# Stick-breaking block of a decoder trunk: prompt heads in two lanes with their own temporaries, transposes laid later behind their scores, 12 page places for 14, columns spread over more steps

## The chip, the cores and the metric

The kernel runs on one core of a Trainium2 chip. The metric is device time in microseconds (us); three unprofiled runs before the change gave 1417.66 us (median), 1416.6 and 1419.02. One more execution was profiled: it took 1419.73 us, and its recorded span, on which every row below is dated, is 1418.0 us.

## The reference, cut to what matters

Two layers run for a prompt group (256 tokens) and a sample group (8 sequences of 8 new tokens). Layer 1 is stick-breaking attention with 16 heads of 64. The samples also attend to a paged cache: 8 pages of 128 past keys each, for each of the 8 sequences.

```python
def sb_block(qb, k, v, q_pos, bias):
    k_pos = jnp.arange(k.shape[1])
    z = jnp.einsum('bqhd,bkhd->bhqk', qb, k).astype(jnp.float32) * (SB_HEAD_DIM ** -0.5)
    z = z + bias.astype(jnp.float32)[None, :, None, None]
    mask = k_pos[None, :] < q_pos[:, None]
    log_rem = jnp.where(mask, jax.nn.log_sigmoid(-z), 0.0)
    rev = lax.cumsum(log_rem, axis=3, reverse=True)
    suffix = jnp.concatenate([rev[..., 1:], jnp.zeros_like(rev[..., :1])], axis=-1)
    att = jnp.where(mask, jnp.exp(jax.nn.log_sigmoid(z) + suffix), 0.0)
    return jnp.einsum('bhqk,bkhd->bqhd', att.astype(v.dtype), v)
...
def odd_mixer(h, w_in, w_out, bias, k_past, v_past):
    b, t, _ = h.shape
    qkv = (h @ w_in).reshape(b, t, 3, SB_HEADS, SB_HEAD_DIM)
...
    return y.reshape(b, t, MIX_WIDTH) @ w_out, k, v
```

## The kernel before, in words

Prompt and sample tokens lie side by side as 320 columns of features. A **column** is one block of 128 output features of a projection: its 512 KB of weights (`raw`) come by one DMA, ScalarE copies them to a rounded high part (`whi`), VectorE forms the low part (`wlo`), and TensorE runs 24 matmuls (8 blocks of features, three products each). `convert_ahead` converts one column ahead of the one that is multiplied and lets `raw` be fetched up to three columns ahead.

`odd_in` first projects the 8 columns of q. Then it walks 18 **steps** `i`. Step `i` does `score` of half sequence `i` (4 key pages, 32 small matmuls into bank `ps`, which the profile shows as two passes each, x64), whose stick-breaking weights (`stick`, a chain over ScalarE and VectorE that ends in an exponential) end up in `s_z`; `value` of half `i-2` (4 value pages, 16 matmuls or x32 in the profile, into `po`); then some of the 16 remaining columns of k and v (`column`; those of v are transposed afterwards by three transposes of `s_vT`); `turn`, which transposes `s_z` of half `i-1` and copies it to `s_at`; and pieces of the prompt's own attention.

How many columns step `i` does is set by `int(COLS * (i + 1))`. The prompt's attention comes in pieces made by `prompt(qb, t0)` and one `new_keys` (the samples' own new keys). A prompt piece does its scores on TensorE (bank `pp`), leaves a chain of some two dozen instructions to ScalarE and VectorE for its two halves in the scratch tile `room`, and yields `LP`, an amount of planned TensorE time after which `steps()` takes the lane up again: four transposes of each half, and 16 value matmuls. `steps()` compares with `pe[0]`, the planner's sum of TensorE time, so `LP` sets the place in TensorE's order, not a time on the chip. In the kernel before there is one lane: a piece begins when the one ahead of it has ended.

The order on TensorE and on SP (the queue that issues the DMAs) is that of the code; on VectorE, ScalarE and GpSimd a scheduler lays it at build time. Each engine works through its own list in order.

The cache comes as 128 **pages** of 512 KB (64 of keys, 64 of values), in the order in which the steps take them. The `PGS` places `pg` are used again and again; nine pages more are put once into tiles that are idle until then (`lend`: `sb_v` 3, `sb_k` 2, `ahi` and `alo` 2 each). Up to `PGS` + 9 pages are fetched before the block starts. From then on `refill` issues the next page in the list right after the matmuls that read a place, and SP waits there for these matmuls. A `raw` is issued from the same queue, behind the pages of its step.

After step 17 the output projection `out_proj` starts (8 columns, `pd`).

Of the kernel before, what the change touches and what calls it, by code (L numbers as in the profile page):

```python
# [10 lines left out]
F32 = mybir.dt.float32  # L11
# [187 lines left out]
def trunk(ctx: ExitStack, tc: tile.TileContext, A, O, phases=None):  # L199
# [26 lines left out]
    def bank(tag="pb", n=None):  # L226
        return own[0].tile([128, 512], F32, tag=tag, name=tag, bufs=n or 5 - own[1])
# [15 lines left out]
    def cc(name):  # L243
        if name in coff:
            at, n = coff[name]
            return cst[:, at:at + n]
        for off, t in (eoff, cste), (soff, csto):
            if name in off:
                at, n = off[name]
                return t[0][:, at:at + n]  # L250
# [3 lines left out]
    def vv(name, i=0, n=1):  # L254
        at, _ = voff[name]
        return vec[:, at + i:at + i + n]
# [12 lines left out]
    def spend(k, m, n, passes):  # L269


        now = (32 if k <= 32 else 64 if k <= 64 else 128, 32 if m <= 32 else 64 if m <= 64 else 128)
        if passes == 0:
            pe[0] += n / 2400 + 0.014
        else:
            pe[0] += passes * max(now[1] / 1200 + 0.004, n / 1200) / (2 if now[1] == 64 else 1)
        if now != shape[0]:
            pe[0] += 0.09
        shape[0] = now

    def mm(out, lhsT, rhs, start=True, stop=True):
        n, m = math.prod(rhs.shape[1:]), math.prod(lhsT.shape[1:])
        spend(lhsT.shape[0], m, n, 0 if lhsT.dtype == F32R else 2)
        nc.tensor.matmul(out, lhsT=lhsT, rhs=rhs, start=start, stop=stop, skip_group_check=True)  # L284

    def tr(out, in_, base=0):
        n = in_.shape[0]
        spend(n, math.prod(in_.shape[1:]), n, 1)
        nc.tensor.transpose(out, in_, ident[base:base + n, base:base + n])
# [3 lines left out]
    def act(out, in_, f=AF.Copy, **kw):  # L293
        if load[0] is not None and f in (AF.Ln, AF.Exp):
            with tc.issue_after(load[0].ins):
                S.activation(out, in_, f, **kw)  # L296
        else:
            S.activation(out, in_, f, **kw)  # L298
# [15 lines left out]
    def stt(out, in0, scalar, in1, op0, op1, eng=None):  # L314
        (eng or V).scalar_tensor_tensor(out, in0=in0, scalar=scalar, in1=in1, op0=op0, op1=op1)  # L315
# [91 lines left out]
    def split(dst, src, scale=1.0):  # L407

        hi, lo = dst
        act(hi, src, scale=scale)  # L410
        stt(lo, src, scale, hi, ALU.mult, ALU.subtract)

    def part(a, *ix):
        return a[0][ix], a[1][ix]
# [1249 lines left out]
    def odd_plan():  # L1664
        return [(A["w_sb"][c], KT) for c in list(range(8)) + [8 * j + t for t in range(8) for j in (1, 2)]] + [(A["w_so"][c], KT) for c in range(KT)]

    PGS = 14
    COLS = 1.8
    GATE = 3
    LP = 9.0  # L1670
    HPO = 300

    class Odd:
# [3 lines left out]
        def __init__(self):  # L1677
            self.made, self.tiles = 0, {}
            self.turn, self.more, self.limit = 0, [], PGS
            self.pool = tc.tile_pool(name="kvr", bufs=1, reuse_waits="tile")  # L1680
# [29 lines left out]
        def fetch(self):  # L1710
# [5 lines left out]
            if lent:  # L1716
                t = self.once.pop(0)
            elif len(self.more) and self.turn >= PGS:
                t = self.more[self.turn - PGS]
            else:  # L1720
                t = self.kvr.tile([128, 1024], F32, tag="pg", name="pg", bufs=PGS)
            if not lent:
                self.turn = (self.turn + 1) % (PGS + len(self.more))
            reg = nc.sync.value_load(pages[0:1, 8 * b + j:8 * b + j + 1], min_val=0, max_val=A["kv"].shape[0] - 1)
# [19 lines left out]
    def odd_in(od, prep, op, ctx):  # L1744
        halves = od.halves
        a = prep.a
        kT, vt = od.kT, od.vt
        qT = op.tile([128, KT, NT], F32, name="sb_q")

        room = op.tile([128, 4, 1024], F32, name="sb_room")  # L1750
        acc = op.tile([128, 8, 64], F32, name="sb_acc")
        new = op.tile([128, KT, 64], F32, name="sb_new")
        ec = op.tile([128, KT, 64], F32, name="sb_ec")
# [6 lines left out]
        st = {}  # L1760
# [5 lines left out]
        def softplus(z, e, l):  # L1766

            act(e, z, AF.Abs)
            act(e, e, AF.Exp, scale=-1.0)
            act(l, e, AF.Ln, bias=1.0)  # L1770
            stt(e, z, 0.0, l, ALU.max, ALU.add)

        def weigh(z, T):
            V.tensor_sub(z, z, T)
            act(z, z, AF.Exp)

        def stick(z, e, l, n, initial=0.0):


            softplus(z, e, l)  # L1780
            one = bc(ones[:, 0:1], [128, n])
            for s in range(0, 512, n):
                V.tensor_tensor_scan(l[:, s:s + n][:, ::-1], data0=one, data1=e[:, s:s + n][:, ::-1],
                                     initial=initial, op0=ALU.mult, op1=ALU.add)
            weigh(z, l)
# [66 lines left out]
            split(part(o, ALL, ALL, slice(NP + 8 * b, NP + 8 * b + 16)), w)  # L1852


        def two(i, p):
            return room[:, i, 512 * p:512 * p + 512]

        def keys(t):
            V.tensor_mul(kT[:, t], dense(a), prep.norm.r)
# [8 lines left out]
                tr(pt[:, tb], vT[:, 128 * tb:128 * tb + 128])  # L1868
            act(vt[:, :, 128 * t:128 * t + 128], pt)

        def prompt(qb, t0):

            n = 128 * (qb + 1)
            H = 512 // n
            qs = slice(128 * qb, 128 * qb + 128)
            rows = [slice(64 * p, 64 * p + 64) for p in range(2)]
            ps = [bank("pp", 2).rearrange("p (h n) -> p h n", h=H) for p in range(2)]
            for j in range(H):
                for p in range(2):
                    mm(ps[p][:, j], qT[rows[p], t0 + j, qs], kT[rows[p], t0 + j, :n])  # L1880
            for p in range(2):
                z = two(0, p).rearrange("p (h n) -> p h n", h=H)
                for j in range(H):
                    b = vv("sb_bias", 2 * (t0 + j) + p)
                    if qb:
                        act(z[:, j, :128], ps[p][:, j, :128], AF.Identity, bias=b)
                    stt(z[:, j, n - 128:], ps[p][:, j, n - 128:], b, cc("causal"), ALU.add, ALU.add)
                stick(two(0, p), two(1, p), two(2, p), n)
            yield LP
            for p in range(2):  # L1890
                pt = bank("pp", 2)
                for j in range(4):
                    s = slice(128 * j, 128 * j + 128)
                    tr(pt[:, s], two(0, p)[:, s])
                act(two(3, p), pt)
                yield 1.0 + p
            py = bank("pp", 2)[:, :128 * H].rearrange("p (t n) -> p t n", n=128)
            for j in range(H):
                for kb in range(qb + 1):
                    for p in range(2):  # L1900
                        h, s = 2 * (t0 + j) + p, n * j + 128 * kb
                        mm(py[rows[p], j], vt[:, kb, 64 * h:64 * h + 64], two(3, p)[:, s:s + 128],
                           start=kb == 0, stop=kb == qb)
            split(part(o, ALL, slice(t0, t0 + H), qs), py)

        def new_keys():

            ps = bank("pp", 2).rearrange("p (t q) -> p t q", t=KT)
            rows = [slice(64 * p, 64 * p + 64) for p in range(2)]
            for t in range(KT):  # L1910
                for p in range(2):
                    mm(ps[rows[p], t], kT[rows[p], t, NP:], qT[rows[p], t, NP:])
            z, e, l = (two(i, 0) for i in range(3))
            for t in range(KT):
                stt(z[:, 64 * t:64 * t + 64], ps[:, t], vv("sb_two", t), cc("win"), ALU.add, ALU.add)
            softplus(z, e, l)
            yield 6.0
            T, all_ = bank("pp", 2), bank("pp", 2)
            mm(T, cc("sufx"), e)
            mm(all_, cc("two64"), e)  # L1920
            weigh(z, T)
            act(ec.rearrange("p t q -> p (t q)"), all_, AF.Exp, scale=-1.0)
            yield 2.0
            pn = bank("pp", 2).rearrange("p (t q) -> p t q", t=KT)
            for t in range(KT):
                for p in range(2):
                    h = 2 * t + p
                    mm(pn[rows[p], t], vt[rows[p], 2, 64 * h:64 * h + 64], z[rows[p], 64 * t:64 * t + 64])
            act(new, pn)
            st["new"] = True  # L1930

        def small():

            for at, g in ((4, prompt(1, 0)), (8, prompt(1, 2)), (8, prompt(0, 0)), (12, prompt(1, 4)),
                          (16, new_keys()), (16, prompt(1, 6)), (16, prompt(0, 4))):
                while st["cols"] < at or st["step"] < GATE:
                    yield None
                yield from g

        lanes = [[small(), 0.0]]  # L1940

        def steps():

# [33 lines left out]
        for i in range(len(halves) + 2):  # L1977
# [7 lines left out]
            if "new" in st:  # L1985
                while ends:
                    finish(ends.pop(0))
            n = max(0, min(16, int(COLS * (i + 1))) - st["cols"])
            steps()
# [77 lines left out]
```

## Time and profile before

| what | value |
|---|---|
| median of 3 runs | 1417.66 us |
| profiled execution, its own time | 1419.73 us |
| span of the profile | 1418.0 us |
| TensorE busy | 1313.9 us (93%) |
| VectorE busy | 901.8 us (64%) |
| ScalarE busy | 661.8 us (47%) |
| DMA | 268.11 MB, mean 189 GB/s |
| scores of step 0 begin | 834.14 us |
| output projection begins | 1046.02 us |

The busy shares are averages over the span. The block that is changed lies between 834 and 1046 us, and what holds it up is read from that stretch alone: which engine waits, for whom, and how busy the DMA engines are. An idle TensorE also shows a lower granted clock afterwards (1.00 in the rows is 2.4 GHz, and a stretch that mixes 2.4 and 1.2 GHz shows a mean between).

### The profile page before, as it was taken

How to read it: one execution, taken by the hardware profiler on the slowest of the kernel's cores; microseconds unless marked ns; L12 is line 12 of the kernel's file. 1: busy time of each engine (PE TensorE's matmuls, PEld its weight loads, DVE VectorE, ACT ScalarE, POOL GpSimd, SP SyncE). 2: the span in 40 equal slices, each digit the busy share in tenths (PEclk: the TensorE clock that was granted, in tenths of full speed). 3: DMA queues.
4: the chain of work that ended last, by engine and by line, in shares of the span. 5: the costliest groups of instructions: out<-in, count | busy, mean ns of one | idle time of the engine just before them, and what ended most of it. 6: DMA issues, size and time to landing. Idle time of an engine off the chain costs nothing.

```text
span 1418.0 us, 28483 instructions
## 1 busy us (share of the span) xinstructions
PE 1313.9 (93%) x10883; PEld 1199.4 (85%) x10883; DVE 901.8 (64%) x1830; ACT 661.8 (47%) x1450; POOL 281.0 (20%) x558
## 2 busy tenths in 40 slices
PE   7799898999999999999999998788689999999997
PEld 6688687887889968999999997676478689999997
DVE  6877787778756545666565656666655455665654
ACT  6645355455436424544344535556444245443443
POOL 6524535435121101111010110000010011110001
PEclk9899998999999999999999999899899999999999
DMA  5333232224437883444757748797997834444443
GB/s 207 119 104 99 89 94 81 87 82 141 145 123 275 309 307 98 152 149 149 249 167 251 269 152 314 253 321 281 408 384 303 299 110 150 149 149 149 149 141 104
DMA packets 81691, 268.11 MB, mean 189 GB/s; under 512 B 9426, under 2 KB 22226, under 8 KB 77074
## 3 DMA queue, kind: packets, MB, share of 16 engines
q1 hardware_dynamic: 64594, 247.30, 50.9%
q10 hardware_dynamic: 16960, 18.98, 4.1%
q8 instruction: 86, 1.41, 0.4%
q14 instruction: 51, 0.42, 0.1%
HBM read 254.35 MB, written 11.90 MB: 188 GB/s over the span
## 4 chain that ended last, share of the span: by engine, by line
PE 60%; DMA 6%; DVE 4%; ACT 3%; issue 1%; SPq 1%; POOL 0%; ACTq 0%; DVEq 0%; POOLq 0%
PE pd L284 33%; PE pe L284 18%; PE pb L284 3%; PE ps L284 2%; DMA mkv<-in_mkv 2%; DMA pg<-in_kv 2%; DMA raw<-in_w_sb 1%; DMA out_memv<-kvt 1%; DVE wlo L358 1%; PE pG L284 1%; PE pR L284 1%; ACT sb_room L296 1%; DVE sb_room L315 1%; PE pp L284 1%; ACT whi L298 1%
## 5 line engine op out<-in xcount | busy, mean ns | idle before, releaser
L298 ACT ACTIVATE whi<-raw 128x512 fp32r<-128x512 f32 (+1 forms) x541 | 308.1, 617 | 381.9 <-PE pd L284 158.9
L358 DVE TENSOR_TENSOR wlo<-raw,whi 128x512 fp32r<-128x512 f32 (+1 forms) x541 | 383.8, 747 | 83.5 <-ACT whi L298 82.1
L284 PE MATMUL pd<-ahi,whi 128*128 128x320 f32 (+2 forms) x1336 | 431.2, 324 | 4.0 <-DVE r_e L1372 1.8
L284 PE MATMUL pd<-ahi,wlo 128*128 128x320 f32 (+1 forms) x1328 | 411.1, 310 | 3.1 <-DVE wlo L358 3.0
L284 PE MATMUL pd<-alo,whi 128*128 128x320 f32 (+2 forms) x1336 | 410.3, 309 | 0.0
L284 PEld LDWEIGHTS pd<-ahi,whi 128*128 128x128 f32 (+1 forms) x1336 | 257.7, 193 | 14.3 <-ACT R L296 2.3
L284 PEld LDWEIGHTS pd<-ahi,wlo 128*128 128x128 f32 x1328 | 257.0, 194 | 5.8 <-DVE wlo L358 4.3
L284 PEld LDWEIGHTS pd<-alo,whi 128*128 128x128 f32 (+1 forms) x1336 | 256.8, 192 | 0.4
L284 PE MATMUL pe<-alo,whi 128*128 128x320 f32 x416 | 129.7, 312 | 0.0
L284 PE MATMUL pe<-ahi,wlo 128*128 128x320 f32 x416 | 129.1, 310 | 0.5 <-DVE wlo L358 0.5
L284 PE MATMUL pe<-ahi,whi 128*128 128x320 f32 x416 | 128.7, 310 | 0.0
L533 POOL TENSOR_TENSOR fw<-fw 128x320 f32<-128x320 f32 x44 | 39.1, 888 | 332.8 <-DVE fw L532 303.5
L434 POOL TENSOR_TENSOR acc<-acc,w 128x320 f32<-128x320 f32 (+1 forms) x48 | 47.7, 994 | 248.2 <-ACT w L298 245.8
L284 PEld LDWEIGHTS pe<-ahi,wlo 128*128 128x128 f32 x416 | 78.1, 188 | 1.5 <-DVE wlo L358 1.4
L284 PEld LDWEIGHTS pe<-alo,whi 128*128 128x128 f32 x416 | 78.1, 188 | 0.5
L284 PEld LDWEIGHTS pe<-ahi,whi 128*128 128x128 f32 x416 | 78.0, 188 | 0.3
L284 PE MATMUL pd<-flo,whi 128*128 128x320 f32 x176 | 54.3, 309 | 0.0
L284 PE MATMUL pe<-fhi,wlo 128*128 128x320 f32 x176 | 54.3, 309 | 0.0
L284 PE MATMUL pd<-fhi,whi 128*128 128x320 f32 x176 | 54.3, 309 | 0.0
L284 PE MATMUL pd<-fhi,wlo 128*128 128x320 f32 x176 | 54.3, 309 | 0.0
L284 PE MATMUL pe<-fhi,whi 128*128 128x320 f32 x176 | 54.3, 309 | 0.0
L284 PE MATMUL pe<-flo,whi 128*128 128x320 f32 x176 | 54.3, 309 | 0.0
(463 smaller groups left out, 2114.0 us busy)
## 6 DMA issues: line engine op xcount, KB each, us to landing
pg<-in_kv SPq DMA_DIRECT2D x119, 512.0 KB, 7.6
raw<-in_w_fi SPq DMA_DIRECT2D x88, 512.0 KB, 3.5
mkv<-in_mkv SPq DMA_DIRECT2D x32, 1024.0 KB, 9.9
raw<-in_w_fo SPq DMA_DIRECT2D x32, 512.0 KB, 3.6
raw<-in_w_sb SPq DMA_DIRECT2D x24, 512.0 KB, 6.8
raw<-in_w_gp SPq DMA_DIRECT2D x16, 512.0 KB, 3.5
raw<-in_w_mk SPq DMA_DIRECT2D x16, 512.0 KB, 3.8
raw<-in_w_mv SPq DMA_DIRECT2D x16, 512.0 KB, 3.6
```

The source lines that it names most:

```text
L284: nc.tensor.matmul(out, lhsT=lhsT, rhs=rhs, start=start, stop=stop, skip_group_check=True)
L296: S.activation(out, in_, f, **kw)
L298: S.activation(out, in_, f, **kw)
L315: (eng or V).scalar_tensor_tensor(out, in0=in0, scalar=scalar, in1=in1, op0=op0, op1=op1)
L358: V.tensor_sub(lo[:, ks], raw[:, ks], hi[:, ks])
L434: P.tensor_add(self.acc, self.acc, self.sq)
L533: P.tensor_mul(u, u, st["g"])
```

## The change

`PGS` goes from 14 to 12, `COLS` from 1.8 to 1.34, `GATE` (the first step in which a prompt piece may start) from 3 to 2, `LP` from 9.0 to 22.0. The one scratch tile `room` of four parts becomes two of three parts (the transposed weights now overwrite a part that is no longer needed), and there are two lanes that draw pieces from one list. The scratch memory of a partition is the same in sum (8 KB more for the scratch tiles, 8 KB less for places).

```diff
-    PGS = 14
-    COLS = 1.8
-    GATE = 3
-    LP = 9.0
+    PGS = 12
+    COLS = 1.34
+    GATE = 2
+    LP = 22.0
...
-        room = op.tile([128, 4, 1024], F32, name="sb_room")
+        rooms = [op.tile([128, 3, 1024], F32, name=f"sb_room{i}") for i in range(2)]
...
-        def two(i, p):
-            return room[:, i, 512 * p:512 * p + 512]
+        def halves_of(room):
+            return lambda i, p: room[:, i, 512 * p:512 * p + 512]
...
-        def prompt(qb, t0):
+        def prompt(qb, t0, two):
...
-                act(two(3, p), pt)
+                act(two(1, p), pt)
...
-        def small():
-
-            for at, g in ((4, prompt(1, 0)), (8, prompt(1, 2)), (8, prompt(0, 0)), (12, prompt(1, 4)),
-                          (16, new_keys()), (16, prompt(1, 6)), (16, prompt(0, 4))):
-                while st["cols"] < at or st["step"] < GATE:
+
+        jobs = [(4, prompt, 1, 0), (8, prompt, 1, 2), (8, prompt, 0, 0), (12, prompt, 1, 4), (16, new_keys),
+                (16, prompt, 1, 6), (16, prompt, 0, 4)]
+
+        def small(room):
+            while jobs:
+                if st["cols"] < jobs[0][0] or st["step"] < GATE:
                     yield None
-                yield from g
-
-        lanes = [[small(), 0.0]]
+                    continue
+                _, f, *x = jobs.pop(0)
+                yield from f(*x, halves_of(room))
+                yield 0.0
+
+        lanes = [[small(room), 0.0] for room in rooms]
```

The columns of k and v by step were 1, 2, 2, 2, 2, 1, 2, 2, 2 (steps 0 to 8); they are now 1, 1, 2, 1, 1, 2, 1, 1, 2, 1, 1, 2 (steps 0 to 11).

On TensorE, at the end of step 1 and the start of step 2, the program before had this (`s_z` with `cst` is `turn`, `pd` is a column of which only the first matmul is shown, `s_vT` are the transposes behind a column of v, `ahi` and `alo` here are lent pages of keys, `po` is `value`):

```order
L289 MATMUL ps<-cst,s_z 128x128 x4
L284 MATMUL pd<-ahi,whi 128x320
...
L289 MATMUL p_10081<-cst,s_vT 128x128 x3
L284 MATMUL ps<-ahi,sqz_9556 32x128 x16
L284 MATMUL ps<-alo,sqz_9556 32x128 x16
L284 MATMUL po<-pg,s_at 32x256 x16
```

The changed program has there:

```order
L289 MATMUL ps<-cst,s_z 128x128 x4
L284 MATMUL ps<-ahi,sqz_9535 32x128 x16
L284 MATMUL ps<-alo,sqz_9535 32x128 x16
L284 MATMUL po<-pg,s_at 32x256 x16
L289 MATMUL p_10133<-cst,s_vT 128x128 x3
```

One column moved from step 1 to step 2, behind the first `value`.

On TensorE around the second prompt piece, `prompt(1, 2)`, the program before had its scores (`pp` from `sb_k`), one score and one value of the samples, and then the piece's first transposes (`pp` from `sb_room`):

```order
L284 MATMUL pp<-sb_k,sb_q 128x256 x4
L284 MATMUL ps<-pg,sqz_9555 32x128 x32
L284 MATMUL po<-pg,s_at 32x256 x16
L289 MATMUL pp<-cst,sb_room 128x128 x4
...
L289 MATMUL ps<-cst,s_z 128x128 x4
L289 MATMUL pp<-cst,sb_room 128x128 x4
```

The changed program has (9529 and 9530 are the scratch tiles of the two lanes; a column is left out behind `s_vT`):

```order
L284 MATMUL pp<-sb_k,sb_q 128x256 x4
L284 MATMUL pp<-sb_k,sb_q 128x128 x8
L284 MATMUL ps<-pg,sqz_9535 32x128 x32
L284 MATMUL po<-pg,s_at 32x256 x16
L289 MATMUL p_11118<-cst,s_vT 128x128 x3
...
L289 MATMUL ps<-cst,s_z 128x128 x4
L284 MATMUL ps<-pg,sqz_9535 32x128 x32
L284 MATMUL po<-pg,s_at 32x256 x16
L289 MATMUL pp<-cst,sb_room_9529 128x128 x4
L289 MATMUL pp<-cst,sb_room_9530 128x128 x4
```

The scores of two pieces now stand together, and a column, a turn and a second score and value lie between them and the transposes. The pieces `(1, 0)` and `(1, 4)` got the same distance, each alone.

On ScalarE at the same piece, the program before mixed one piece (`sb_room`) with the score's chain (`s_e`, `s_l`):

```order
L298 ACTIVATE sb_room<-pp,vec 128x128 x3
L298 ACTIVATE sb_room<-sb_room 128x512
L296 ACTIVATE sb_room<-sb_room 128x512
L298 ACTIVATE s_e<-s_z 128x512
L298 ACTIVATE sb_room<-sb_room 128x512
L296 ACTIVATE sb_room<-sb_room 128x512
L296 ACTIVATE s_e<-s_e 128x512
L296 ACTIVATE sb_room<-sb_room 128x512
L296 ACTIVATE s_l<-s_e 128x512
L296 ACTIVATE sb_room<-sb_room 128x512 x2
```

The changed program has both pieces ahead of the score's chain:

```order
L298 ACTIVATE sb_room_9529<-pp,vec 128x128 x4
L298 ACTIVATE sb_room_9529<-sb_room_9529 128x512 x2
L296 ACTIVATE sb_room_9529<-sb_room_9529 128x512 x4
L298 ACTIVATE sb_room_9530<-sb_room_9530 128x512
L296 ACTIVATE sb_room_9530<-sb_room_9530 128x512
L298 ACTIVATE sb_room_9530<-sb_room_9530 128x512
L296 ACTIVATE sb_room_9530<-sb_room_9530 128x512 x3
L298 ACTIVATE whi<-raw 128x512 x2
L296 ACTIVATE sb_room_9529<-sb_room_9529 128x512 x2
L298 ACTIVATE s_e<-s_z 128x512
```

Six instructions of the second piece came to stand between the first piece's softplus and its closing exponentials.

## Rows read from the trace of the kernel before

**Rows 1.** Busy time by stretch: PE, PEld, DVE, ACT, POOL, PE clock, DMA share, GB/s.
```profile
851.00:972.04 121.04, 100.41 (x1199) 88.80 (x1199) 76.08 (x137) 66.15 (x127) 7.33 (x23) 0.92 0.80 286
...
972.04:1046.02 73.98, 54.83 (x915) 37.37 (x911) 48.12 (x96) 39.47 (x73) 3.57 (x12) 0.88 0.99 387
...
980.00:1000.00 20.00, 14.16 (x264) 10.01 (x256) 14.85 (x27) 12.50 (x25) 1.45 (x5) 0.86 1.02 406
```

**Rows 2.** TensorE's waits from 851.00 to 972.04: us in total, times, longest.
```profile
PE pp L289 <- ACT sb_room L296: 17.3, 3, 7.8
PE pp L284 <- DVE alo L315: 2.6, 3, 1.5
PE po L284 <- ACT s_at L298: 0.7, 1, 0.7
```

**Rows 3.** TensorE in order of time, steps 1 to 3: start, us, instruction.
```profile
846.62 0.60 PE L289 MATMUL ps<-cst,s_z 128*128 128x128 f32 x4
846.98 0.39 PE L284 MATMUL pd<-ahi,whi 128*128 128x320 f32 x1
...
850.58 0.49 PE L289 MATMUL p<-cst,s_vT 128*128 128x128 f32 x3
851.00 1.08 PE L284 MATMUL ps<-ahi,sqz 128*32 128x128 f32 x32
...
862.61 1.95 PE L284 MATMUL ps<-pg,sqz 128*32 128x128 f32 x64
864.38 1.91 PE L284 MATMUL po<-pg,s_at 128*32 128x256 f32 x32
866.22 1.13 PE L284 MATMUL pp<-sb_k,sb_q 64*128 64x256 f32 x8
867.29 0.42 PE L284 MATMUL pd<-ahi,whi 128*128 128x320 f32 x1
```

**Rows 4.** TensorE in order of time, prompt pieces; in brackets idle time and releaser.
```profile
883.78 0.66 PE L289 MATMUL pp<-cst,sb_room 128*128 128x128 f32 x4 [3.90 <-ACT sb_room L296]
...
897.23 1.95 PE L284 MATMUL ps<-pg,sqz 128*32 128x128 f32 x64
...
906.48 1.11 PE L289 MATMUL pp<-cst,sb_room 128*128 128x128 f32 x4 [5.57 <-ACT sb_room L296]
...
947.59 1.96 PE L284 MATMUL ps<-pg,sqz 128*32 128x128 f32 x64
...
959.56 1.11 PE L289 MATMUL pp<-cst,sb_room 128*128 128x128 f32 x4 [7.82 <-ACT sb_room L296]
...
969.94 1.09 PE L284 MATMUL pp<-sb_room,sb_v 128*64 128x128 f32 x16
970.96 1.15 PE L284 MATMUL pp<-sb_q,sb_k 64*64 64x64 f32 x32
972.04 1.19 PE L284 MATMUL ps<-pg,sqz 128*32 128x128 f32 x36
```

**Rows 5.** Busy time by stretch, one column each, as in group 1.
```profile
867.29:870.91 3.62, 3.62 (x26) 3.61 (x25) 2.48 (x5) 2.40 (x5) 0.00 (x0) 1.00 0.80 230
...
907.24:913.20 5.96, 5.96 (x26) 5.96 (x25) 2.66 (x5) 1.83 (x3) 0.00 (x0) 0.56 1.01 380
```

**Rows 6.** SP in order of time, the last burst of page issues.
```profile
972.75 60.65 SPq L1725 DMA_DIRECT2D pg<-in_kv  x50
```

**Rows 7.** The chain that ended last, its pieces at the block's end.
```profile
1042.83 0.68 PE po L284 x8
...
1046.02 14.07 PE pd L284 x85
```

**Rows 8.** DMA issues from 851.00 to 972.04: KB each, median us to landing.
```profile
raw<-in_w_sb SPq DMA_DIRECT2D x10, 512.0 KB, 9.0
```

**Rows 9.** ScalarE's waits from 834 to 1047.
```profile
ACT whi L298 <- DMA raw<-in_w_sb: 13.0, 5, 4.1
```

**Rows 10.** Groups of instructions by shape, 834 to 1047: busy us, mean ns.
```profile
L296 ACT ACTIVATE sb_room<-sb_room 128x512 f32<-128x512 f32 x39 | 23.6, 623 | 7.3 <-DVE sb_room L1774 7.1
```

More of the change, by code (lines that the diff above doesn't have):

```diff
@@ L1901, in prompt, with new_keys @@
                         h, s = 2 * (t0 + j) + p, n * j + 128 * kb
-                        mm(py[rows[p], j], vt[:, kb, 64 * h:64 * h + 64], two(3, p)[:, s:s + 128],
+                        mm(py[rows[p], j], vt[:, kb, 64 * h:64 * h + 64], two(1, p)[:, s:s + 128],
                            start=kb == 0, stop=kb == qb)
             split(part(o, ALL, slice(t0, t0 + H), qs), py)
-        def new_keys():
+        def new_keys(two):
             ps = bank("pp", 2).rearrange("p (t q) -> p t q", t=KT)
```

## The prediction

> **What bounds the kernel now.** I read the busy time by stretch first, for the block alone [rows 1]. It falls into two parts. From 851.00 us (score of step 2) to 972.04 us (score of step 9) the DMA engines are busy 80% and move 286 GB/s, and TensorE works 100.41 of 121.04 us at a mean clock of 0.92: neither is full. From 972.04 to 1046.02 us the DMA share is 0.99, and inside it runs at 406 GB/s: that part is bound by page transfers. So time is lost in the first part, because DMA has capacity there that the second part pays for. The reader should see in the 0.80 and the 0.99 that a stall of TensorE costs time only before 972 us.
>
> The waits of TensorE say for whom [rows 2]: of the 20.6 us idle, 17.3 us are three waits of the prompt's transposes (`pp`) for the closing exponential of `sb_room`. The order of time shows them [rows 4]: 3.90, 5.57 and 7.82 us. Behind the waiting transposes stand a column, a turn, the next score and the next value in TensorE's list, and behind the latter two stand the pages: SP reissues a place only when its matmuls are done. So a stalled transpose also holds up DMA. A second price is the clock: a column takes 3.62 us at clock 1.00, and the one behind the 5.57 us wait took 5.96 us at 0.56 [rows 5], that is mostly at 1.2 GHz.
>
> **What a step costs TensorE when nothing stalls** [rows 3, 4], from start to start: a column 3.60 us (846.98 to 850.58), a turn 0.36 (846.62 to 846.98), the transposes behind a column of v 0.42 (850.58 to 851.00), a score 1.77 (862.61 to 864.38), a value 1.84, a piece's scores 1.07, its value matmuls 1.02 (969.94 to 970.96), the scores of `new_keys` 1.08. Four transposes of a piece I price like a turn.
>
> Test on the program before, score of step 2 to score of step 9: 13 columns 46.8, 7 scores 12.4, 7 values 12.9, 7 turns 2.5, 6 v-transposes 2.5, 4 piece scores 4.3, 8 piece transposes 2.9, 4 piece values 4.1, `new_keys` 1.1: 89.5 us. It took 121.0. Of the 31.5 us lost, 20.6 are idle and 10.9 are lower clock, 0.53 us for each us idle.
>
> **The change, part by part.**
>
> *Columns spread (COLS).* One column with its v-transposes leaves the place ahead of step 2's score, so this score starts at 847.0 us, not 851.00. The last column now comes in step 11. From the score of step 2 to that of step 12 the new order has 14 columns 50.4, 10 scores 17.7, 10 values 18.4, 10 turns 3.6, 7 v-transposes 2.9, 5 piece scores 5.4, 8 piece transposes 2.9, 4 piece values 4.1, `new_keys` 1.1: 106.5 us. Without a stall step 12 begins at 953.5. In the same work the steps now release pages more often: ten steps where seven went.
>
> *Transposes later (LP) and two lanes.* In the three stalled cases the weights were ready 16.5 us (867.29 to 883.78), 9.3 us (897.23 to 906.48) and 12.0 us (947.59 to 959.56) after the piece's scores [rows 3, 4]. The new order puts score, value, v-transposes, column, turn, score and value between: 11.6 us. For the two pieces that stand alone in this part I take the middle of 9.3 and 16.5, 12.9 us, so 1.3 us of stall each, 2.6 together (ends 0 and 9.8). The pair `(1, 2)` and `(0, 0)` has 12.7 us (11.6 and the second scores), but ScalarE does the second piece's 8 activations largely ahead of the first one's last, 8 times 0.623 us [rows 10], 5.0: 17.9 less 12.7 is 5.2 us of stall (ends 0, and 13.0 if a long and a short chain follow one another whole, 25.7). The samples' own score waits in the same queues; if its bank is freed late, TensorE stands at the next score in place of the transposes, and the 5.2 covers that too. The other waits of [rows 2], 3.3 us, stay. Idle 11.1 us, clock 0.53 of it, 5.9: step 12 begins at 953.5 + 17.0 = 970.5 us. (Ends: no stall beyond the 3.3, and 26.1 us idle with 13.8 of clock, 993.4.)
>
> *Page transfers.* A page takes 524288 bytes / 406 GB/s = 1.29 us. Before, the score of step 9 found 78 pages issued; 50 were issued from 972.75 on [rows 6], and the value matmuls of the last began at 1042.83 [rows 7], 70.8 us after the score's start: 64.5 of transfer and 6.3 of lead-in and gaps. In the new order 28 pages are issued behind step 12's score. That is 22 fewer: 70.8 - 28.4 = 42.4 us. The block then ends 3.2 us later, as before (1042.83 to 1046.02). 970.5 + 42.4 + 3.2 = 1016.1 us.
>
> *Is DMA that far by then?* From step 3's score on (847.0 + 12.7 for step 2 = 859.7) 100 pages and 12 `raw` are issued: 112 x 1.29 = 144.5 us, with 6.3 of lead-in 1010.5, and 3.2 more: 1013.7. This is the floor that no order of TensorE's work goes under; it lies 2.4 us under the sum, so the two limits nearly meet.
>
> *Two places fewer (PGS).* Two pages less are fetched ahead, 2.6 us of transfer, which is counted in the 100 and the 28. Twelve places still hold 15.5 us of transfer, and the new steps take 106.5 / 10 = 10.7 us without stalls, 12.4 with: the queue should not run dry. *GATE* only lets the first piece begin in step 2. Scratch memory that is reused inside a piece adds no instruction.
>
> A rule speaks against this part. The Trainium skill, Perfetto Trace Analysis, section Optimization Strategy, says that bubbles which repeat on the engine that should be saturated can mean too little memory for the next tile, the number of buffers among it; by it fewer places would bring the bubbles back (the second rival gives the time). Another of its pages, DMA: Bandwidth & Descriptors, section Where 436 GB/s comes from, lets reads from HBM be bound at about 358 GB/s; 112 transfers would take 164 us by it and the block would end at 1033, an estimate from that page of about 1405 us. The trace disagrees, with 406 GB/s over 20 us.
>
> Behind the block TensorE's order is the same row for row, and it is busy without longer gaps, so I carry the gain through whole: 1046.0 - 1016.1 = 29.9 us. The profiled execution (1419.73, span 1418.0) becomes 1389.8; its median of unprofiled runs lies 2.1 us lower, so 1417.66 - 29.9 = 1387.8.
>
> **The rivals.**
>
> *Two lanes clog ScalarE and VectorE.* In the first part VectorE is busy 76 of 121 us, 63% [rows 1]. The same work in less time makes that some 80%, and the lists are in order. If every piece waits as long as the upper ends above, step 12 begins at 993.4, the block ends at 1039.0, and the time is 1410.7. For it speaks the ScalarE order of the pair. Against it: 9.3 us in one of the three old cases, and a longer distance now.
>
> *Twelve places starve the queue.* If the first part stays at its old 286 GB/s, a transfer takes 1.83 us. The 64 pages and 9 `raw` up to the keys of step 12 then take 133.8 us, these arrive at 999.8, the block ends at 1045.4, and the time is 1417: no change. For it: the three steps with two columns and a piece take up to 14.8 us before any stall, near the 15.5 us that twelve places hold. Against it: the old idle share has a cause that is removed, steps of 17.3 us on average (121.0 / 7).
>
> *Late weights, the other side.* A `raw` stands behind the 8 pages of its step, and now behind a queue that is always full. It landed 9.0 us after its issue [rows 8]; behind 12 pages it would be 15.5. ScalarE waited 13.0 us in five waits for `raw`, at most 4.1 [rows 9], and everything behind `whi` in its list waits along. There are 14 such columns: the gain is gone when each holds up TensorE by 29.9 / 14 = 2.1 us more. At the 4.1 us of the longest, 57.4 - 13.0 = 44.4 us are added and the time is 1387.8 + 44.4 = 1432. Against it: a `raw` is fetched three columns ahead, 3 x 7.6 = 22.8 us in the new order.
>
> *The waits were cover.* If DMA decided the block's end anyway, the stalls would be free and nothing would change. The 0.80 of [rows 1] excludes this: some 24 us of DMA time stand idle in the first part.
>
> **Chances.** Forecast (1383 to 1394): 0.58. Clogged queues (1394 to 1412): 0.26. Better than the floor allows, from less lead-in: 0.05. Starved queue, no change: 0.05. Late weights, slower: 0.06. 0.2% of the time, 2.8 us, is about what a measurement here can tell from no change: faster 0.89, same 0.05, slower 0.06. The range for 8 in 10 goes from 1382 (the floor with half its lead-in) into the clogged case, to 1404; the forecast's own range is 1383 to 1394.
>
> **What would show it.** In the new profile: score of step 2 at about 847; the waits of `pp` for `sb_room` down from 17.3 to about 8 us up to step 12; columns near 3.6 us at clock 1.00; step 12's score near 970; DMA share from 860 on above 0.95; the output projection at about 1016. It would be wrong if DMA shows idle slices between page bursts of 12, if TensorE waits for `whi`, `wlo` or `raw`, or if transposes still wait 4 us and more.

## The result, and the profile after

The changed kernel took 1397.99 us (median of 4 runs, 1395.14 to 1402.58) where the kernel before took 1418.34 us on the same chip: a ratio of 0.9834, 95% interval 0.9812 to 0.9856. That is 20.4 us less. The forecast was 1387.8; the time lies inside the range of 1382 to 1404, but above the forecast's own range of 1383 to 1394. The profiled execution took 1397.65 us, its span 1395.8 us, 22.2 us less than before.

Busy time by stretch, of the changed kernel, columns as in [rows 1]. The first two rows answer to the two parts of the block; step 12 is where the prediction cut it. Then the whole block, a column (for [rows 5]), and the stretch behind the longest wait.
```profile
847.84:972.88 125.04, 112.16 (x1535) 94.74 (x1534) 91.03 (x164) 75.85 (x146) 11.56 (x33) 0.99 0.99 377
972.88:1022.94 50.06, 35.54 (x604) 25.45 (x603) 35.29 (x72) 29.88 (x59) 2.40 (x2) 0.90 0.98 370
...
834.84:1022.94 188.10, 159.55 (x2317) 131.01 (x2316) 133.97 (x247) 112.24 (x214) 17.58 (x44) 0.96 0.94 357
...
864.43:868.03 3.60, 3.60 (x27) 3.60 (x26) 1.74 (x5) 3.53 (x7) 0.00 (x0) 1.00 0.92 261
912.57:916.07 3.50, 3.50 (x33) 1.39 (x33) 2.95 (x5) 1.62 (x3) 2.46 (x5) 0.52 1.04 420
```

The same row for the whole block of the kernel before:
```profile
834.14:1046.02 211.88, 170.94 (x2317) 140.83 (x2316) 135.62 (x247) 113.88 (x214) 15.31 (x45) 0.91 0.84 311
```

These two rows hold the whole gain. The block is 211.88 - 188.10 = 23.8 us shorter, with the same 2317 matmuls. TensorE's busy time fell by 11.4 us, most of it by the clock (170.9 x 0.91 / 0.96 = 162.0, where 159.6 were measured), and its idle time fell from 40.9 to 28.6 us, by 12.4. Ahead of the block 0.7 us and behind it 0.9 us were lost, which leaves the 22.2. Not every part of the block got shorter: from the score of step 12 to the output projection the kernel before took 47.2 us (998.86 to 1046.02), the changed one 50.1.

TensorE's waits in the first part, 847.84 to 972.88, and below them those in the tail, 972.88 to 1022.94 (us in total, times, longest). They answer to [rows 2].
```profile
PE po L284 <- ACT s_at L298: 8.8, 3, 4.6
PE pp L284 <- DVE sb_room L315: 2.9, 2, 1.7
PE ps L284 <- DVE s_z L319: 0.6, 1, 0.6
PE po L284 <- DMA pg<-in_kv: 0.3, 1, 0.3
...
PE pp L284 <- ACT sb_new L298: 4.1, 1, 4.1
PE po L284 <- ACT s_at L298: 2.7, 3, 1.8
PE pp L289 <- DVE s_w L1849: 2.0, 1, 2.0
PE pp L289 <- DVE sb_room L315: 1.9, 1, 1.9
PE pp L284 <- DVE s_w L1849: 1.8, 1, 1.8
PE pp L284 <- DVE sb_acc L1839: 0.9, 1, 0.9
```

The 17.3 us that the prompt's transposes (L289) waited for the closing exponential are gone from the first part. A new wait stands in their place: the value matmuls (`po`) of the samples wait for `s_at`, ScalarE's copy of the transposed weights. In the tail no row names a page. TensorE there is idle for 14.5 of 50 us, and what it waits for are ends of chains on ScalarE and VectorE, or copies that stand behind them.

TensorE in order of time at the pair of pieces, and then in the tail, answering to [rows 4]: start, us, instruction, and in brackets the idle time ahead of it.
```profile
904.84 0.60 PE L289 MATMUL ps<-cst,s_z 128*128 128x128 f32 x4
906.06 1.95 PE L284 MATMUL ps<-pg,sqz 128*32 128x128 f32 x64 [0.62 <-DVE s_z L319]
...
912.57 3.57 PE L284 MATMUL po<-pg,s_at 128*32 128x256 f32 x32 [4.56 <-ACT s_at L298]
916.07 1.09 PE L289 MATMUL pp<-cst,sb_room 128*128 128x128 f32 x8
...
985.77 0.48 PE L284 MATMUL pp<-sb_k,sb_q 64*128 64x128 f32 x2
990.39 1.52 PE L284 MATMUL pp<-sb_k,sb_q 64*128 64x128 f32 x14 [4.14 <-ACT sb_new L298]
```

By the kernel's code the copy to `s_at` needs only the turn, and its tile back from the value before, which had ended at 901. The turn began on TensorE at 904.84 and was done at 905.4, yet the copy ran at 911.94. ScalarE and then VectorE in order of time show why:
```profile
907.60 0.63 ACT L296 ACTIVATE s_l<-s_e 128x512 f32<-128x512 f32 x1
910.37 0.63 ACT L296 ACTIVATE sb_room<-sb_room 128x512 f32<-128x512 f32 x1 [2.14 <-DVE sb_room L1774]
910.90 1.13 ACT L298 ACTIVATE whi<-raw 128x512 fp32r<-128x512 f32 x2
911.94 0.57 ACT L298 ACTIVATE s_at<-ps 128x512 f32<-128x512 f32 x1
...
905.92 1.36 DVE L1783 TENSOR_TENSOR_SCAN sb_room<-cst,sb_room 128x128 f32<-128x128 f32 x4
907.20 1.26 DVE L358 TENSOR_TENSOR wlo<-raw,whi 128x512 fp32r<-128x512 f32 x2
908.39 1.36 DVE L1783 TENSOR_TENSOR_SCAN sb_room<-cst,sb_room 128x128 f32<-128x128 f32 x4
909.67 0.66 DVE L1774 TENSOR_TENSOR sb_room<-sb_room 128x512 f32<-128x512 f32 x1
```
In ScalarE's list the copy stands behind a closing exponential of piece `(0, 0)`. This exponential waits for VectorE, which is busy 18.53 of the 20 us from 900 to 920 and does eight scans of the piece and two low parts of weights (`wlo`) first. So a copy that could have run waits behind a chain that it doesn't depend on. TensorE waits 4.56 us, and the value behind the wait then runs 3.57 us at a granted clock of 0.52, mostly at 1.2 GHz, where another takes 1.9 [rows 3]. The longest wait of the tail looks the same: the matmuls in front of the copy to `sb_new` ended at 985.8, and the copy ran at 989.76, behind exponentials that had waited for VectorE.

SP's last burst of page issues and what follows it, answering to [rows 6], and the pieces of the chain that ended last, which in [rows 7] went through the last value matmuls:
```profile
973.58 38.67 SPq L1725 DMA_DIRECT2D pg<-in_kv  x28
1012.35 0.38 SPq L2007 DMA_DIRECT2D out_sbk<-sb_k  x1
...
1013.34 12.79 DMA out_sbv<-sb_v
...
1026.74 6.45 DMA raw<-in_w_so
...
1034.69 5.40 PE pd L284 x35
```
The 28 pages of the prediction are there, one every 1.38 us. At the block's end the critical chain no longer runs through the last value: it runs through the write of `sb_v`, behind which SP issues the projection's weights.

### The profile page after: what moved, and what is told of

Its sections match the earlier page's. It is cut to its first block, busy times and chain, and to the rows that moved or that the text cites. A ratio compares the mean times of both kernels' runs of the same rounds, so it can differ in the third digit from the quotient of the medians.

```text
span 1395.8 us, 28468 instructions
## 1 busy us (share of the span) xinstructions
PE 1303.1 (93%) x10883; PEld 1189.4 (85%) x10883; DVE 899.0 (64%) x1830; ACT 660.3 (47%) x1450; POOL 281.5 (20%) x558
## 5 line engine op out<-in xcount | busy, mean ns | idle before, releaser
L284 PEld LDWEIGHTS pd<-ahi,whi 128*128 128x128 f32 (+1 forms) x1336 | 254.8, 191 | 14.5 <-ACT R L296 2.3
L284 PEld LDWEIGHTS pd<-ahi,wlo 128*128 128x128 f32 x1328 | 254.2, 191 | 8.0 <-DVE wlo L358 6.6
```

## Experiments

Two questions were asked. First: which part of the change makes the gain? Theory A says the distance between a piece's scores and its transposes, which only two lanes can afford; its rival B says the spread columns alone. Second: where did the rest of the forecast gain go? Theory 1 says that chains in the lists of ScalarE and VectorE hold the end; Theory 2 that the twelve places do, because pages arrive late. The first four kernels shared a chip, so did the next four and the last four, and each ratio is to the kernel before on that chip. The changed kernel, run a second time beside the last group, had 0.9867 [0.9836, 0.9897], and its block took 190.4 us in place of 188.1: differences under 3 us between two experiments tell nothing. The expected times were written beside 1418 us for the kernel before; on the three chips it took 1421.6, 1423.0 and 1421.9 us.

### Parts of the change alone

**Only the spread columns** (in the kernel before):
```diff
-    COLS = 1.8
+    COLS = 1.34
```


> The kernel before with COLS 1.34 alone (14 places, one lane, distance 9). Theory A: the gain of the change comes from the distance between a prompt piece's scores and its transposes, which two lanes make affordable; spreading columns alone keeps the short distance, so the waits of the transposes for the scratch tile stay above 12 us, and the last piece slides behind step 17, in front of the output projection: no gain, 1412 to 1425. Rival B: the gain comes from pages being released more evenly when columns are spread, with DMA busy from 860 us on; then this alone gives most of it, 1395 to 1403.

Measured: 1420.95 us, ratio 0.9992 [0.9967, 1.0017]. Score of step 2 came 13.0 us after that of step 0, as in the changed kernel, but the transposes' waits stay, 18.9 us in three (first row below), and the last piece's transposes came behind the last value, which started at 1031.1 (second row).
```profile
PE pp L289 <- ACT sb_room L296: 18.9, 3, 8.4
...
1037.99 1.12 PE L289 MATMUL pp<-cst,sb_room 128*128 128x128 f32 x4 [2.98 <-ACT sb_room L296]
```
B falls: spreading columns alone brings nothing.

**Only the later transposes:**
```diff
-    LP = 9.0
+    LP = 22.0
```


> The kernel before with LP 22 alone. A: the three waits of the transposes before 972 us (17.3 us) vanish, score of step 9 near 955 instead of 972, but in one lane the pieces last longer, two of them stand behind step 17 and TensorE waits for their chains in front of the output projection, 15 to 25 us: 1405 to 1425. B: distance matters little: within 4 us of before with the same DMA share before 972 us.

Measured: 1428.54 us, ratio 1.0046 [1.0024, 1.0068]: slower, also than A had it. No transpose waited before step 10's score (964.2 us), though the scores of the next piece waited 10.3 us there for the piece ahead to empty its bank (`alo`). With one lane the pieces are put off one behind the other. The last value started 193.9 us after the first score, where the kernel before took 206.7, and a piece was still to come, with its full wait:
```profile
1050.49 1.12 PE L289 MATMUL pp<-cst,sb_room 128*128 128x128 f32 x4 [7.41 <-ACT sb_room L296]
```

**Everything but the two lanes and the places** (one lane, 14 places):
```diff
-    COLS = 1.8
-    GATE = 3
-    LP = 9.0
+    COLS = 1.34
+    GATE = 2
+    LP = 22.0
```


> Spread columns, distance 22 and GATE 2 in one lane with 14 places. A: up to step 12 like the changed kernel (score of step 12 near 970), two pieces behind step 17 cost 15 to 25 us more at the end: 1402 to 1420. B: DMA feed is all that counts, lanes do nothing, and two places more even help: 1392 to 1398.

Measured: 1421.21 us, ratio 0.9991 [0.9962, 1.002]. The time is 1 us above A's range. The last value started 179.6 us after the first score (at 1017.1), 4 us sooner than in the changed kernel (183.6), but pieces were left over. TensorE's waits from there to 1052 us:
```profile
PE pp L289 <- ACT sb_room L296: 8.3, 2, 7.4
PE pp L284 <- DVE s_w L1849: 4.4, 2, 4.2
PE pp L289 <- DVE s_w L1849: 2.5, 2, 2.2
```
All that the first part gains is given back behind the last step.

**Only the two lanes and twelve places** (in the changed kernel the other three numbers of before):
```diff
-    COLS = 1.34
-    GATE = 2
-    LP = 22.0
+    COLS = 1.8
+    GATE = 3
+    LP = 9.0
```


> The changed kernel with COLS 1.8, LP 9, GATE 3 again: two lanes and 12 places alone. A: the transposes still come too early and two pieces share ScalarE and VectorE, so their waits for the scratch tiles reach 20 to 30 us up to the last column: 1415 to 1425. B: 1405 to 1412, since the pieces end earlier.

Measured: 1436.51 us, ratio 1.0109 [1.0062, 1.0156]: slower. Waits from 850 to 1055 us:
```profile
PE pp L289 <- ACT sb_room L296: 13.6, 3, 7.4
PE pp L289 <- ACT sb_ec L296: 6.1, 1, 6.1
PE po L284 <- DMA pg<-in_kv: 5.2, 9, 0.8
```
This is slower than A had it, too. A second lane without the distance lets more chains wait in the same lists; what the two places fewer add isn't separated here (all waits for pages are 7.0 us in this stretch, where the kernel before had 4.7). So no part gains alone, two of them lose, and the whole gains 1.7%. That the lanes are what lets every piece have its distance and still be done before the last step, as A says, is borne out by a run further down: with fourteen places, the same columns and distance and two lanes (the tiles shared) the ratio is 0.9848, with one lane it was 0.9991. No run has two lanes and the distance without the spread columns, so whether these are needed beside them isn't shown.

### What holds the rest: lists or places

**Two pieces without their chains.** In the changed kernel the pieces `(1, 6)` and `(0, 4)` keep only their scores, a copy and the write; bias, softplus, scan, transposes and value matmuls are left out.
```diff
-                (16, prompt, 1, 6), (16, prompt, 0, 4)]
+                (16, stub, 1, 6), (16, stub, 0, 4)]
```


> The changed kernel with the last two prompt pieces, (1, 6) and (0, 4), cut to their score matmuls, a copy out of the banks and a write of these scores in place of the result: bias, mask, softplus, scans, exponentials, transposes and value matmuls of the two are left out. Theory 1 (the end of the block is held by the pieces' chains in the in-order lists of ScalarE, VectorE and TensorE, not by pages): output projection 45 to 47 us after the score of step 12 instead of 50.1, time 1391 to 1395. Theory 2 (12 places cannot keep pages coming, the chains are cover): still 49 to 51 us, time 1396 to 1400.

Measured: 1402.46 us, ratio 0.987 [0.9812, 0.9928]: no gain that can be told, though work was left out. The tail alone took 47.0 us, 3.0 less than in the changed kernel and at the edge of what Theory 1 expected. But the scores of `(0, 4)` now come ahead of step 12's score, and the first part took 130.4 us in place of 125.0 (with them, and at a mean clock of 0.96 for 0.99). The block took 190.4 us, as long as that of the changed kernel run again. In the tail the waits for chains fell from 13.4 to 4.5 us, and pages came up behind them with 6.2:
```profile
PE po L284 <- DMA pg<-in_kv: 4.9, 8, 1.1
PE po L284 <- ACT s_at L298: 3.6, 3, 1.7
PE ps L284 <- DMA pg<-in_kv: 1.3, 2, 0.7
PE pp L284 <- DVE sb_acc L1839: 0.9, 1, 0.9
```
So Theory 1 alone is not enough: with the chains gone, TensorE waits for pages, and the block is not shorter.

**Ten places:**
```diff
-    PGS = 12
+    PGS = 10
```


> The changed kernel with 10 places instead of 12. Theory 1: two pages less ahead, 2.6 us of transfer, time 1399 to 1403 and DMA share up to step 12 still above 0.93. Theory 2: ten places hold 12.9 us of transfer, less than the longest steps, so DMA idles in them, share below 0.90 and time 1408 to 1418.

Measured: 1406.34 us, ratio 0.9893 [0.9843, 0.9943]; the block took 195.0 us, where those of the kernels with twelve took 188.1 to 192.8. The time lies between the two theories; the DMA share in the first part was 0.97, as Theory 1 had it. Waits in the first part:
```profile
PE po L284 <- DMA pg<-in_kv: 10.0, 17, 0.7
PE po L284 <- ACT s_at L298: 3.0, 2, 2.2
PE pp L284 <- DVE sb_room L315: 2.9, 2, 1.7
```
Waits for pages rose from 0.3 to 10.3 us, and the waits for `s_at` fell from 8.8 to 3.0: the one is partly the cover of the other. At this point two places cost some 5 us (the two kernels with twelve that follow took 1401.11 and 1401.23 us on the same chip). Beside the changed kernel's block of 188.1 us it looked like 7, and I took that for support of Theory 2, with some 3 us for each place.

**The pair taken apart.** Piece `(0, 0)` is let in from 10 columns on, not 8:
```diff
-(8, prompt, 0, 0)
+(10, prompt, 0, 0)
```


> The changed kernel with piece (0, 0) started two columns later, so that no two pieces begin together before step 11. Theory 1: the wait of the value matmuls for the copied turn (4.6 us) and the waits for banks around the pair (1.7 and 0.6 us) go, score of step 2 to score of step 12 takes 120 to 122 us instead of 125.0, if DMA (0.99 busy there) lets it; time 1394 to 1397. Theory 2: DMA is the limit of that part already, so the waits move to pages: 124 to 126 us and 1397 to 1400.

Measured: 1401.11 us, ratio 0.9853 [0.9802, 0.9905], no difference from the changed kernel that can be told. The first part took 125.3 us where it had taken 125.0, as Theory 2 expected. The waits for `s_at` fell to 4.2 us, those for `sb_room` rose from 2.9 to 5.2, and 1.9 us of pages came.

**Pieces earlier and in another order** (gates 3, 6, 7, 11, 15, 15, 15):
```diff
-        jobs = [(4, prompt, 1, 0), (8, prompt, 1, 2), (8, prompt, 0, 0), (12, prompt, 1, 4), (16, new_keys),
-                (16, prompt, 1, 6), (16, prompt, 0, 4)]
+        jobs = [(3, prompt, 1, 0), (6, prompt, 0, 0), (7, prompt, 1, 2), (11, prompt, 1, 4), (15, prompt, 0, 4),
+                (15, new_keys), (15, prompt, 1, 6)]
```


> The changed kernel with every piece allowed one column earlier and in the order (1,0), (0,0), (1,2), (1,4), (0,4), new_keys, (1,6), so that pairs no longer begin together and one of the last two pieces is done earlier. Theory 1: both parts get shorter, output projection at 1016 to 1019, time 1391 to 1395. Theory 2: 1396 to 1400.

Measured: 1401.23 us, ratio 0.9849 [0.98, 0.9898]. In the first part `s_at` cost 0.2 us and pages 5.3; in the tail 14.8 us of waits for chains remained. The output projection began 191.9 us after the first score, later than Theory 1 had it. Again much the same sum in other names.

**Fourteen places, and their control.** Room for two more places was made by letting the two halves of a piece share their intermediate tiles; the control has the sharing and twelve places.
```diff
-        rooms = [op.tile([128, 3, 1024], F32, name=f"sb_room{i}") for i in range(2)]
+        rooms = [op.tile([128, 4, 512], F32, name=f"sb_room{i}") for i in range(2)]
...
-            return lambda i, p: room[:, i, 512 * p:512 * p + 512]
+            return lambda i, p: room[:, (p, 2, 3, 2 + p)[i]]
```
The transposed result takes part 3 in place of 1. Control, `PGS = 12`:

> The changed kernel, with the two halves of a piece sharing their intermediate halves of the room (e and l), and the transposed result in their place: 8 KB a partition less, 12 page places as in the changed kernel. The second half of a piece now has to wait for the first one's last use of e and l; everything else stays. Both theories: within 3 us of the changed kernel (1395 to 1401 beside a kernel before of 1418), the time from the first score to the last value 183 to 188 us against 184.9. It is the control for the next one.

With `PGS = 14`:

> The same with 14 page places. Theory 2 (the twelve places hold the block back: the rate falls whenever few transfers are outstanding, and each place is worth some 3 us; from the first score to the last value 208.7 us in the kernel before, 191.8 with 10 places, 184.9 with 12, 179.6 with 14 places and one lane): 5 us shorter than with 12 (1390 to 1395, ratio about 0.981), first score to last value 179 to 181 us, the DMA rate in the stretch from step 2 to step 12 near 390 GB/s where the changed kernel had 377. Theory 1 (the chains in ScalarE's and VectorE's lists hold the end): no gain over the 12 places, first score to last value 184 to 187 us, the waits for s_at and sb_room as they were. The forecast's own price (1.29 us for each place): 2.6 us shorter.

Measured: 1399.06 us, ratio 0.9846 [0.9816, 0.9877] with twelve places, and 1400.99 us, ratio 0.9848 [0.9815, 0.9881] with fourteen. The blocks took 192.8 and 189.2 us, the changed kernel beside them 190.4. With fourteen places TensorE waited for no page at all, neither in the first part, whose two rows stand here, nor in the tail:
```profile
PE po L284 <- ACT s_at L298: 7.5, 4, 3.5
PE pp L284 <- DVE sb_room L315: 2.9, 2, 1.7
```
The time stayed: by the means of six runs each, the two places more cost 0.4 us, give or take some 3.5. Theory 2's gain of 5 us is excluded; the forecast's own price, 2.6 us, is not (the two blocks differ by 3.6, in one execution each). The rate from step 2 to step 12 was 374 GB/s with twelve and with fourteen, not near 390. So Theory 2 falls too as it was stated: only 0.3 to 0.7 us of waits for pages were left to buy in the first part. My 3 us for each place came from the ten places, where places do bind, and from the early last value of the one-lane kernel, which is early because work was put behind it. Its 179.6 us, moreover, count to the last value's first matmul and the others to its last page; counted like them it is 180.9. The control's own time to the last value, 189.7 us, was longer than expected (183 to 188).

**Fourteen places and the pair taken apart:**
```diff
-    PGS = 12
+    PGS = 14
...
-(8, prompt, 0, 0)
+(10, prompt, 0, 0)
```
(with the shared tiles)

> 14 places, shared halves, and the piece (0,0) let in from 10 columns on where it was 8, so that it no longer runs beside (1,2). Theory 2: pages bind less with 14 places, so that the 4.6 us that the value waits for s_at at the pair (1,2) with (0,0) is now worth something: 0 to 3 us shorter than the 14 places alone (1388 to 1394). Theory 1: 4 to 5 us shorter than the 14 places alone.

Measured: 1405.72 us, ratio 0.9879 [0.984, 0.9917], and a block of 195.5 us. Neither theory expected it longer. Its interval overlaps with the others', so that it is slower isn't shown; that it isn't 4 us faster is. The waits for `s_at` fell to 4.5 us in the first part and those of the pieces for `sb_room` rose to 8.2.

**The changed kernel again**, as the measure for this group:

> The changed kernel itself beside the others on one chip: ratio to the kernel before 0.981 to 0.986, as measured; first score to last value 184 to 186 us. It tells what 12 shared and 14 shared places are compared with.

Measured: 1403.66 us, ratio 0.9867 [0.9836, 0.9897], and 187.2 us from the first score to the last value: both a little above what was expected of a repetition (0.981 to 0.986, 184 to 186). No variant beat it by more than its interval.

## Why the prediction was right, and where it was off

**Score of step 2 at 847.0.** It came at 847.84; from step 0's score 13.00 us, where 12.86 were worked out. Right.

**The first part, 123.5 us.** It took 125.04. TensorE was busy 112.16 us, where 106.5 of work and 5.9 of clock make 112.4; it was idle 12.9 where the sum had 11.1. A column took 3.60 us at clock 1.00, as priced. That the busy time agrees is partly luck. The clock was 1.00 in this part but for the stretch behind the longest wait, where it cost the value some 1.7 us, not 5.9. The other 4 us are turns, transposes, scores and columns that took a little longer than their prices. The 0.53 for each us idle had put down to the clock all lost time that was not idle; a mean clock of 0.92 over 100.41 us [rows 1] explains about 8.0 of those 10.9 us. Of the idle time the size was nearly right and the owner wrong in part: I gave 7.8 us to transposes waiting for `sb_room`, and no transpose waited. The 5.2 us for the pair turned up as 4.56 us at the value of the next step. The prediction had named the score's bank as the other place where it could come out; it was the copy of the turn, held up in ScalarE's list.

**The tail, 45.6 us: the term that was mis-sized.** It took 50.06. The prediction counted 28 pages at the full rate to the last value, 42.4 us, and no wait of TensorE; the value came after 46.9. The count of pages was right. But the tail wasn't bound by pages: TensorE waited for none of them, and stood 12.5 us ahead of the last value for ends of chains (`sb_new`, `s_at`, `s_w`, `sb_room`). Its clock was 0.90 in the mean. The places came free late, and SP issued a page every 1.38 us in place of 1.29 (once it stood 4.2 us for a place). In the second part of the kernel before (972.04 to 1046.02) both limits had been at work; pages were waited for there, 3.9 us ahead of values and 0.8 ahead of scores, beside the closing exponentials:
```profile
PE pp L289 <- ACT sb_room L296: 6.5, 2, 3.9
PE po L284 <- DMA pg<-in_kv: 3.9, 7, 0.7
```
I had worked out that the two limits nearly meet (2.4 us apart) and then let the DMA alone set the tail; no term of the sum priced TensorE's own busy time and waits there, 35.5 and 14.5 us. The runs show a trade between the two. Without two chains 6.2 us of pages come up; with fourteen places no page is waited for, and chains hold the block at 189.2 us beside the 190.4 of the changed kernel; with ten, 10.3 us of pages replace 5.8 of `s_at` in the first part.

**Two places fewer, 2.6 us.** The queue did not run dry at twelve, as said (0.3 us of waits in the first part); at ten it does. So the rival of the starved queue, and the rule on repeated bubbles in the Trainium skill, Perfetto Trace Analysis, Optimization Strategy, have their point one step further down than this change goes: the trace agrees with the rule at ten places (18 waits for pages in the first part, of 0.7 us at most), not at twelve (one).

**The rate.** I set 406 GB/s against the 358 of the Trainium skill, DMA: Bandwidth & Descriptors, Where 436 GB/s comes from. The two parts ran at 377 and 370 GB/s in the mean, and single stretches at 410 (hardware section below), so 358 is not the limit here. The estimate worked out from this figure of the Trainium skill, 1405 us, lies nearer to the measured 1398 than the 1385 that the floor of 1013.7 gives, but that is chance: the means are low because stretches at 331 to 352 GB/s lie between others at 410, and TensorE waited for pages only 0.3 us in the first part and not at all in the tail.

**The gain carried through whole.** It lost 0.9 us behind the block (372.9 us in place of 372.0): TensorE waited 3.4 us for `wlo` in the first 54 us of the output projection where it had waited 2.1. The chain through the write of `sb_v` and the weights behind it stands with the profile after.

**The rivals.** Late weights hardly came: a `raw` landed 9.0 us after its issue, as before [rows 8] and not 15.5, and ScalarE waited once for one of the k and v columns, 2.9 us, where it had waited 13.0 [rows 9]. That wait lasted until 861.45 and put off the chain of the first piece, whose scores had ended at 860.6, to 862.50; how much of the next wait for `s_at`, 2.88 us at 873.39, is due to it isn't separated. The waits were not mere cover in the kernel as changed, though the later transposes alone show that removing them alone gains nothing. The clogged lists came in a small measure, and they are what went wrong with the sum: the 8.8 us of `s_at` and the waits of the tail, 1.5 and 4.5 us over the sum and not 23.

**The balance.** Of the forecast 29.9 us the profile shows 22.2. The 7.7 us that lack are 0.7 ahead of the block, 0.1 to step 2, 1.5 in the first part, 4.5 in the tail and 0.9 behind. The 0.7 ahead of the block are scatter between executions (last section).

**What stays open.** No run takes away the chains' waits and the pages' together (fourteen places with shorter chains), so how far the block falls when both limits are moved isn't shown. No run moves only the copies that TensorE waits for ahead of the chains in ScalarE's list, so what they alone cost isn't shown either. Nor is it shown what the spread columns add beside two lanes, and why the pair taken apart gained nothing with fourteen places.

## What to carry to other kernels

When a wait is taken away by putting distance in, look for the resource that lets every chain have that distance at once: here the distance alone put work behind the last step and cost 0.5%, the second lane (with two places fewer) cost 1.1%, and both with spread columns gained 1.7%. Where a sum shows two limits within a few us of one another, price the busy time and the waits of both, and check whether removing one wait brings up another, as it did here. Look also at what stands in an in-order list ahead of a short copy that the busiest engine waits for. A busy share of 0.98 on DMA doesn't say that transfers bind: look whether the consumer waits for any.

## What the runs showed of the hardware

DMA's busy share says less of its rate than it seems to. Three stretches of 20 us of the changed kernel, columns as above:
```profile
860.00:880.00 20.00, 17.12 (x264) 14.49 (x261) 13.75 (x26) 13.24 (x27) 1.75 (x5) 1.00 0.93 331
880.00:900.00 20.00, 18.29 (x278) 15.53 (x280) 14.58 (x31) 12.42 (x26) 2.65 (x7) 1.00 1.03 410
...
920.00:940.00 20.00, 20.00 (x304) 17.32 (x302) 10.91 (x19) 11.57 (x24) 1.48 (x7) 1.00 0.97 352
```
A share of 0.97 goes with 352 GB/s and one of 1.03 with 410: the rate is 14% lower and the share 6%.

The part ahead of the block, in which nothing was changed, ended at times from 831 to 843 us in the profiled executions of kernels that differ only in the block, and once each at 834.84 and 842.76 for the changed kernel itself. Times of single executions are compared here from the block's own first score on.
